# Seven products instead of eight on both column pairs of a split-precision MLP, on one core

## The chip, the cores and the metric

The kernel runs on one core of one Trainium2 chip. The number that counts is the time of one execution in microseconds (us), as the device measures it; the kernel before was run three times, and its median is the reference. A profile of one further execution shows each instruction on each engine: TensorE (PE, with its weight loads PEld), VectorE (DVE), ScalarE (ACT), GpSimd (POOL), and SyncE (SP), which here only issues transfers.

## The reference

A decoder trunk of two layers on 256 tokens of width 2048, all in float32. Layer 0 has recurrent mixers, layer 1 a dilated attention; each is followed by an MLP with 8192 hidden columns. The change lies in the MLP and in how weights are brought to the matmuls:

```python
def squared_relu_mlp(h, w1, w2):
    return jnp.square(jax.nn.relu(h @ w1)) @ w2

for layer in range(DEPTH):
    hn = rms_norm(h, norm_mix[layer])
    ...
    h = h + mix
    h = h + squared_relu_mlp(rms_norm(h, norm_mlp[layer]), mlp_w1[layer], mlp_w2[layer])
return rms_norm(h, final_norm)
```

## The kernel before

**Precision by three matmuls.** Each float32 operand is held as two parts, `hi` (the value rounded to the matmul's input type) and `lo` (the rest), and a product is computed as hi·hi + hi·lo + lo·hi. The parts of the activations live in `bufa` and `bufb` (columns 0 to 255 hi, 256 to 511 lo). The parts of the weights are made on the fly by `Weights.split`: ACT casts a loaded block to `hi` (line 105), DVE subtracts it from the raw block to get `lo` (line 106).

**Units.** All weights are cut into units of 128 partitions x 2048 floats, 1 MB each. The list `units` is the order in which PE needs them. `unit` hands out the next one and calls `fetch` for the one two places ahead, which issues the load on SP's queue (line 123) and the split. The raw blocks have 3 buffers (`wraw`); `hi` and `lo` each have 5 half-unit tiles of 128x1024, thus two and a half units. A scheduler sets the order on each engine; `stream()` and `urgent()` give priorities; the order of the main matmuls among themselves is chained by `mm`.

**The MLP.** The 8192 hidden columns are done in four quarters `q`, in both layers. In a quarter, 16 units of `w1` each give one block of 128 hidden features for all tokens (`project`, `cross`: 16 matmuls of 512 columns and 16 of 256); the result is folded, squared after the relu and split into `bufb` (lines 229 to 242 and 684 to 687). Then 16 units of `w2` take the 16 blocks of the quarter to the output: four column blocks `n` of 512 output columns, two token halves `j`, 16 feature blocks `k`.

**The products.** For the first column pair (n = 0 and 1, as `PAIRS = 1`), the first 8 feature blocks are taken as a two-by-two block product in Strassen's manner: with two token halves, two column blocks and pairs of feature blocks there are seven block products of 12 matmuls each instead of eight. They need sums of activations, which `sums` makes into the tile `forms` during the w1 stage (four sums for each of four pairs of blocks, split into hi and lo), and sums of weights, which `combine` makes on DVE (line 147): `a` becomes a+t1, then a+t1+t2, then that plus d; and `t1` becomes t1+t2 for the product called `t3`. The tiles `a` and `t1` have one buffer each in the pool `pair`. The other 8 feature blocks of the pair are done plainly, in the units called `n`, 24 matmuls each. `PRODUCTS` is the order of the eleven units of a pair; `times` runs the matmuls; `to_x` adds a finished bank to the residual `xres` (the tile `xall`) on DVE (line 657) and, in the last quarter, calls the norm's square on ACT (line 295). The second column pair (n = 2 and 3) is done plainly by `tokens` (192 matmuls for 8 units), and `add_res` adds it (line 592).

**Turning the residual.** At the end of the last quarter of layer 0 each of the four 512-column blocks of the residual is transposed by PE, eight transposes of 128x128 (line 186), scaled and split into `bufa` by ACT and DVE (lines 240 and 241) for the attention's projections. `to_features` puts the work on the list `later`; `flush` runs the list after the next unit of matmuls. As `mlp` calls `products` for two column blocks and only then `to_features`, blocks 0 and 1 come into one flush. The transposes have two banks of PSUM, `pl`.

In the built program `forms` lies at byte 182,048 of its partition in layer 0 and at 186,144 in layer 1; neither is a multiple of 64. `bufa`, `bufb`, `hi` and `lo` lie on multiples of 64.

Of the kernel before, what the change touches and what calls it, by code (L numbers as in the profile page):

```python
# [40 lines left out]
def trunk_kernel(ctx, tc, x, xtok, cols, tab, masks, pos, fin, w_in, w_gate, w_out, w_qkv, w_o, w1, w2, out):  # L41
# [2 lines left out]
    cst = pool("cst")  # L44
    act = pool("act")
    wraw = pool("wraw", 3)
    whi = pool("whi", 5)
    wlo = pool("wlo", 5)
    tmp = pool("tmp", 2)
    mixers = ExitStack()  # L50
    pmm = pool("pmm", 3, space=PSUM)
# [6 lines left out]
    xall = act.tile([P, KB * S], F32, name="xall")  # L58
    xin = xall.rearrange("p (k s) -> p k s", s=S)
    xres = xall.rearrange("p (j d) -> p j d", j=2)  # L60
    bufa = act.tile([P, KB, 2 * S], F32R, name="bufa")
    bufb = act.tile([P, KB, 2 * S], F32R, name="bufb")

    units = []
    made = {}
# [1 line left out]
    def plan(src, n):  # L67
        units.extend((src, i) for i in range(n))
# [13 lines left out]
    units.extend((w_out, 4 * n + g) for n in range(4) for g in (2, 3, 0, 1))  # L82
    for layer in range(2):
        if layer:
            plan(w_qkv, 48)
            plan(w_o, 16)
        for q in range(4):
            units.extend((w1, layer * 64 + q * 16 + i) for i in range(16))
            for n in range(0, 4, 2):
                plan2(layer * 64 + q * 16 + 4 * n, n < 2 * PAIRS)  # L90
    at = [0, 0]

    class Weights:
        def __init__(self, raw, now=True):
            self.raw = raw
            self.hi = [whi.tile([P, 1024], F32R, name="hi") for _ in range(2)]
            self.lo = [wlo.tile([P, 1024], F32R, name="lo") for _ in range(2)]
            if now:
                self.split(0, 1024)
                self.split(1024, 1024)  # L100

        def split(self, at, n):
            h, l = self.part(at, n)
# [2 lines left out]
            V.tensor_tensor(l, w, h.bitcast(F32), OP.subtract)  # L106

        def part(self, at, n):
            i, r = divmod(at, 1024)
            return self.hi[i][:, r:r + n], self.lo[i][:, r:r + n]  # L110

    def fetch():
        u = at[0]
        if u >= len(units):
            return
        at[0] += 1
        src, i = units[u][:2]
        with stream():
            if len(units[u]) > 2:
                combine(u, src, i, units[u][2])  # L120
                return
            r = wraw.tile([P, 2048], F32, name="raw")
            nc.sync.dma_start(r, src[i])
            made[u] = Weights(r)

    held = {}

    def combine(u, src, i, what):
        if what in ("a", "t1"):
            r = held[what] = pair.tile([P, 2048], F32, name=what)  # L130
            nc.sync.dma_start(r, src[i])
        elif i is not None:
            r = wraw.tile([P, 2048], F32, name="raw")
            nc.sync.dma_start(r, src[i])
            held[what] = r
        to, add = {"t1": ("a", "t1"), "t2": ("a", "t2"), "t3": ("t1", "t2"), "t4": ("a", "d"),
                   "a": ("a", None), "c": ("t2", None), "d": ("d", None), "n": ("n", None)}[what]
        r = held[to]
        if what == "t3" and T3_DMA:
            nc.gpsimd.dma_start(r, w2[held["c_at"]], accum_op=OP.add)  # L140
            add = None
        if what == "t2":
            held["c_at"] = i
        for h in range(2):
            at = slice(h * 1024, h * 1024 + 1024)
            if add:
                V.tensor_tensor(r[:, at], r[:, at], held[add][:, at], OP.add)
            if h == 0:
                w = made[u] = Weights(r, False)
            w.split(h * 1024, 1024)  # L150

    def fetch_first():
        for u in range(4):
            at[0] += 1
            r = wraw.tile([P, 2048], F32, name="raw")
            src, i = units[u]
            n = (4, 2, 1, 1)[u]
            for m in range(n):
                ks = slice(4 * u + m * 4 // n, 4 * u + (m + 1) * 4 // n)
                ws = slice(m * 2048 // n, (m + 1) * 2048 // n)  # L160
                nc.sync.dma_start(xin[:, ks], x[:, ks])
                nc.sync.dma_start(r[:, ws], src[i][:, ws])
                if m == 0 and n > 1:
                    made[u] = Weights(r, False)
                for k in range(ks.start, ks.stop):
                    split_to(bufa[:, k], xin[:, k], col("nmix0", k))
                if n > 1:
                    made[u].split(m * 2048 // n, 2048 // n)
                else:
                    made[u] = Weights(r)  # L170

    def unit(src, i):
        u = at[1]
# [90 lines left out]
    class FirstNorm:  # L264
# [2 lines left out]

        def add(self, blk):
            self.n += 1
            q = tmp.tile([P, S], F32, name="n1", bufs=2)  # L270
            A.activation(q, blk, AF.Square)
            if self.n == 1:
                self.ss.append(tmp.tile([P, S], F32, name="ssq", bufs=1))
                V.tensor_copy(self.ss[0], q)
            elif self.n < KB:
                V.tensor_tensor(self.ss[0], self.ss[0], q, OP.add)
            else:
                self.ss.append(q)
# [65 lines left out]
            flush()  # L344
        return ps

    def tokens_group(src, i0, rt=None, by_k=False):
        ps = tokens(src, i0, bufa, by_k=by_k)
        v = vgs.tile([P, 2, 512], F32, name="vg", bufs=2)
        with urgent():  # L350
            for j in range(2):
                A.activation(v[:, j], ps[j], AF.Copy, scale=1.0 if rt is None else rt[:, j:j + 1])
        return v
# [73 lines left out]
        scaled(p, z, acc)  # L427
        return z

    vgs = mixers.enter_context(tc.tile_pool(name="vgs", bufs=2))  # L430
    wk = mixers.enter_context(tc.tile_pool(name="wk", bufs=2))


# [92 lines left out]

    def lru_in(b):
        p = project(w_in, b, bufa, XA)
        xp = wk.tile([P, S + 4], F32, name="xp", bufs=2)
        V.memset(xp[:, :4], 0.0)  # L530
        scaled(p, xp[:, 4:], XA)
        A.activation(xc[:, b], xp[:, 4:], AF.Identity, bias=col("conv_b", b), scale=col("conv_w", 24 + b))
        for i in range(3):
            V.scalar_tensor_tensor(xc[:, b], xp[:, 1 + i:1 + i + S], col("conv_w", 8 * i + b), xc[:, b],
                                   op0=OP.mult, op1=OP.add)
        split_to(bufb[:, b], xc[:, b])
# [93 lines left out]
        A.copy(forms[:, k, 0], t)  # L630
        V.tensor_tensor(forms[:, k, 1], t, forms[:, k, 0].bitcast(F32), OP.subtract)

    def products(i0, n0, nrm, r2, r2n):
        n1 = n0 + 1
        i0 += 4 * n0
        plain = lambda j, k: (bufb[:, k, j * P:j * P + P], bufb[:, k, S + j * P:S + j * P + P])
# [28 lines left out]
        for what, u in PRODUCTS:  # L665
            w = unit(w2, None if u is None else i0 + u)
            if what != "n":
                times(bank[what], w, side[what])
                for job in after_product.get(what, ()):
                    to_x(*job)  # L670
                continue
            n, g = divmod(u, 4)
            for j in (1, 0) if n else (0, 1):
                times({(0, 0): gamma, (0, 1): beta, (1, 0): alpha, (1, 1): delta}[n, j], w,
                      lambda i, j=j, g=g: plain(j, 4 * g + i))
                if g == 3:
                    to_x({(0, 0): gamma, (0, 1): beta, (1, 0): alpha, (1, 1): delta}[n, j], j, n + n0, 1, (n, j) != (1, 1))
            flush()

    def mlp(layer, nrm, nxt, gname):  # L680
        r2 = None
        for q in range(4):
            for m in range(16):
# [7 lines left out]
                if r2 is None:  # L691
# [4 lines left out]
                        lut(spare, epsc, AF.Sqrt)  # L696
                    spot[:] = [after(V.memset(spare, 0.0), [])]
            ends = nxt if q == 3 else None
            for n in range(4):
                if n < 2 * PAIRS:  # L700
                    if n % 2 == 0:
                        products(layer * 64 + q * 16, n, ends, r2, r2n)
                else:
                    ps = tokens(w2, layer * 64 + q * 16 + 4 * n, bufb)
                    add_res(ps, n, ends, r2)
                if q == 3:
                    if gname:
                        to_features(n, gname)
                    else:
                        at = slice(n * 512, n * 512 + 512)  # L710
                        with urgent():
                            for j in range(2):
                                V.tensor_tensor(xres[:, j, at], xres[:, j, at], fing[:, at], OP.mult)

    pairs = ExitStack()
    pair = pairs.enter_context(tc.tile_pool(name="pair0", bufs=1))
    forms = pair.tile([P, 4, 2, 512], F32R, name="forms")
    nx1 = Norm()
    mlp(0, nrm, nx1, "nmix1")
    pairs.close()  # L720
# [78 lines left out]
    pend = []  # L799
    for g in range(4):  # L800
        if g < 3:
            vg = tokens_group(w_qkv, g * 12, rt)
        for hd in range(4 * g, 4 * g + 4):
            u0 = g * 12 + (4 if g < 3 else 0) + (hd % 4) * 2
            st = scores(u0)
# [13 lines left out]
    fing = late.tile([P, D], F32, name="fing")  # L819
    nc.sync.dma_start(fing, bass.AP(tensor=fin.tensor, offset=fin.offset, ap=[[0, P], [1, D]]))  # L820
    pair = pairs.enter_context(tc.tile_pool(name="pair1", bufs=1))
    forms = pair.tile([P, 4, 2, 512], F32R, name="forms")
    fnorm = Norm()
    mlp(1, nrm, fnorm, None)
    pairs.close()
    for j in range(2):
# [3 lines left out]
        with urgent():  # L830
# [18 lines left out]
URGENT = 400  # L849
ORDER = "v0 h0 x0 h1 x1 h2 x2 h3 x3 v1 h4 x4 h5 x5 h6 x6 h7 x7 g0 y0 y1 y2 y3 g1 y4 y5 y6 y7"  # L850
WARM = 12
PAIRS = 1
T3_DMA = False
PRODUCTS = (("a", 0), ("t1", 4), ("n", 6), ("t2", 5), ("c", None), ("n", 7), ("t3", None), ("d", 1), ("n", 2),
            ("t4", None), ("n", 3))
NOSYNC = mybir.DependencyInfo(mybir.DependencyClass.NoSync, mybir.DependencyReason.DATA)


# [101 lines left out]
```

## Time and profile before

| | |
|---|---|
| median of 3 runs | 2222.8 us (2221.32 to 2223.05) |
| profiled execution | 2222.9 us, its span from first to last instruction 2221.1 us |
| PE busy | 2201.0 us, 99% of the span, 12100 matmuls and transposes |
| DVE busy | 1603.2 us, 72% |
| ACT busy | 1142.7 us, 51% |
| POOL busy | 1.9 us |
| TensorE clock granted | 0.998 of full speed |
| DMA | 414.53 MB, 187 GB/s in the mean; SP's queue takes 51.6% of the 16 engines' time |

The page of a profile lists busy times, groups of equal instructions (count, busy time, mean duration of one, and the idle time before them with the instruction that ended it), and the chain of work that ended last. A duration in such a row runs from the start of an instruction to its end; as instructions of one engine overlap at their ends, the distance from start to start can be shorter, and for matmuls is much shorter.

### The profile page before, as it was taken

How to read it: one execution, taken by the hardware profiler on the slowest of the kernel's cores; microseconds unless marked ns; L12 is line 12 of the kernel's file. 1: busy time of each engine (PE TensorE's matmuls, PEld its weight loads, DVE VectorE, ACT ScalarE, POOL GpSimd, SP SyncE). 2: the span in 40 equal slices, each digit the busy share in tenths (PEclk: the TensorE clock that was granted, in tenths of full speed). 3: DMA queues.
4: the chain of work that ended last, by engine and by line, in shares of the span. 5: the costliest groups of instructions: out<-in, count | busy, mean ns of one | idle time of the engine just before them, and what ended most of it. 6: DMA issues, size and time to landing. Idle time of an engine off the chain costs nothing.

```text
span 2221.1 us, 30636 instructions
## 1 busy us (share of the span) xinstructions
PE 2201.0 (99%) x12100; PEld 1917.1 (86%) x12100; DVE 1603.2 (72%) x2526; ACT 1142.7 (51%) x1620; POOL 1.9 (0%) x7
## 2 busy tenths in 40 slices
PE   9999999999999999999999999999999999999998
PEld 8999998888888888888788888888888888888886
DVE  7777886578578578578667778556776776785784
ACT  7444485555455455455555445455544554554553
POOL 0000000000000000000000000000000000000000
PEclk9999999999999999999999999999999999999999
DMA  8444446555555554654454454655465455555543
GB/s 311 152 155 169 153 153 236 181 190 193 202 189 183 200 192 169 226 190 148 181 185 170 176 184 159 232 184 184 152 235 198 174 208 194 189 206 190 189 162 123
DMA packets 58720, 414.53 MB, mean 187 GB/s; under 512 B 6528, under 2 KB 7296, under 8 KB 9168
## 3 DMA queue, kind: packets, MB, share of 16 engines
q1 hardware_dynamic: 58320, 412.20, 51.6%
q8 instruction: 95, 1.56, 0.3%
q0 software_dynamic: 256, 0.38, 0.1%
q14 instruction: 49, 0.40, 0.1%
HBM read 410.70 MB, written 2.10 MB: 186 GB/s over the span
## 4 chain that ended last, share of the span: by engine, by line
PE 97%; ACT 1%; DVE 1%; issue 0%; DMA 0%; SPq 0%; ACTq 0%; DVEq 0%
PE p L183 88%; PE pd L183 6%; PE pl L478 1%; PE pl L186 0%; PE pl L774 0%; ACT hi L105 0%; PE po L795 0%; PE pd L787 0%; DMA xall<-in_x 0%; DVE lo L106 0%; DVE bufa L241 0%; ACT L206 0%; ACT bufa L240 0%; PE pd L462 0%; PE pl L773 0%
## 5 line engine op out<-in xcount | busy, mean ns | idle before, releaser
L106 DVE TENSOR_TENSOR lo<-raw,hi 128x1024 fp32r<-128x1024 f32 (+1 forms) x742 | 895.1, 1219 | 474.2 <-ACT hi L105 325.0
L105 ACT CAST hi<-raw 128x1024 fp32r<-128x1024 f32 (+1 forms) x742 | 777.8, 1049 | 776.3 <-PE p L183 660.0
L183 PE MATMUL p<-bufa,hi 128*128 128x512 f32 (+1 forms) x3840 | 858.1, 357 | 2.4 <-DVE bufa L241 2.4
L183 PEld LDWEIGHTS p<-bufa,hi 128*128 128x128 f32 x3840 | 671.6, 189 | 95.0 <-DVE bufa L241 3.8
L183 PE MATMUL p<-hi,bufb 128*128 128x512 f32 x1984 | 621.3, 390 | 0.0
L183 PE MATMUL p<-bufa,lo 128*128 128x256 f32 x3200 | 519.9, 284 | 0.0
L183 PEld LDWEIGHTS p<-bufa,lo 128*128 128x128 f32 x3200 | 451.7, 191 | 12.3
L183 PEld LDWEIGHTS p<-hi,bufb 128*128 128x128 f32 x1984 | 373.1, 188 | 78.4 <-DVE xall L657 1.2
L183 PE MATMUL p<-lo,bufb 128*128 128x512 f32 x992 | 386.5, 390 | 0.0
L183 PEld LDWEIGHTS p<-lo,bufb 128*128 128x128 f32 x992 | 186.5, 188 | 38.2
L183 PE MATMUL p<-hi,bufa 128*128 128x512 f32 x384 | 122.4, 395 | 0.0
L230 ACT COPY t<-p 128x256 f32<-128x256 f32 x128 | 47.6, 372 | 88.7 <-PE p L183 88.7
L105 ACT CAST hi<-a 128x1024 fp32r<-128x1024 f32 x64 | 67.3, 1051 | 46.2 <-PE p L183 20.6
L238 DVE TENSOR_TENSOR bufb<-zp,bufb 128x256 fp32r<-128x256 f32 x128 | 54.2, 423 | 47.1 <-ACT bufb L237 41.3
L183 PEld LDWEIGHTS p<-hi,bufa 128*128 128x128 f32 x384 | 72.1, 188 | 15.5 <-ACT hi L105 0.9
L183 PE MATMUL pd<-hi,bufb 128*128 128x512 f32 x256 | 82.9, 390 | 0.0
L183 PE MATMUL p<-lo,bufa 128*128 128x512 f32 x192 | 76.3, 398 | 1.8 <-DVE lo L106 1.8
L106 DVE TENSOR_TENSOR lo<-a,hi 128x1024 fp32r<-128x1024 f32 x64 | 76.5, 1216 | 0.0
L686 DVE SCALAR_TENSOR_TENSOR zp<-zp 128x256 f32<-128x256 f32 x128 | 54.2, 423 | 3.5
L183 PEld LDWEIGHTS pd<-hi,bufb 128*128 128x128 f32 x256 | 48.1, 188 | 9.8
L237 ACT CAST bufb<-zp 128x256 fp32r<-128x256 f32 x128 | 51.6, 403 | 7.8 <-DVE zp L686 7.8
L232 DVE TENSOR_TENSOR zp<-p,t 128x256 f32<-128x256 f32 x128 | 53.3, 416 | 0.0
(230 smaller groups left out, 1369.8 us busy)
## 6 DMA issues: line engine op xcount, KB each, us to landing
raw<-in_w SPq DMA_DIRECT2D x240, 1024.0 KB, 4.8
raw<-in_w_qkv SPq DMA_DIRECT2D x48, 1024.0 KB, 4.8
raw<-in_w_in SPq DMA_DIRECT2D x46, 1024.0 KB, 4.8
raw<-in_w_out SPq DMA_DIRECT2D x16, 1024.0 KB, 4.8
raw<-in_w_o SPq DMA_DIRECT2D x16, 1024.0 KB, 4.8
a<-in_w SPq DMA_DIRECT2D x8, 1024.0 KB, 4.8
t<-in_w SPq DMA_DIRECT2D x8, 1024.0 KB, 5.5
xall<-in_xtok SPq DMA_DIRECT2D x1, 2048.0 KB, 9.3
```

Of the source, the lines that this page charges most:

```text
L105: A.copy(h, w)
L106: V.tensor_tensor(l, w, h.bitcast(F32), OP.subtract)
L183: chain[:] = [after(T.matmul(*args, **kw), chain)]
L230: A.copy(t, p[:, S:])
L232: V.tensor_tensor(z, p[:, :S], t, OP.add)
L237: A.copy(dst[:, :S], src)
L238: V.tensor_tensor(dst[:, S:], src, dst[:, :S].bitcast(F32), OP.subtract)
L478: T.matmul(pl[:, j], kq[:, js], halves(qp[:, js], c, True), start=True, stop=True)
L686: V.scalar_tensor_tensor(z, z, 0.0, z, op0=OP.max, op1=OP.mult)
```

## The change

1. `PAIRS` goes from 1 to 2: the second column pair of each quarter is done with products too.
2. The order `PRODUCTS` has t4 ahead of the last two plain units, so that both come last.
3. The sum t1+t2 for `t3` is made by a transfer: a DMA on POOL's queue reads the block t2 from memory once more and adds it into the tile `t1` (`accum_op=OP.add`), issued when t2 is fetched.
4. `hi` and `lo` become whole-unit tiles of 128x2048, three buffers each (five halves before). The units of w1 and w2 are cast and subtracted in one instruction of 2048 columns, and weight sums are added in one; units of other weights still in two of 1024.
5. `products` calls `done` for column block n1 after t3 and flushes after t4, and calls it for n0 at its end; so residual blocks are turned singly. The first group of the attention's projections takes its weights in the order 0, 1, 3, 2, as block 3 is now finished ahead of block 2.
6. `forms`, `bufa`, `bufb`, `hi` and `lo` are aligned to 64 bytes: `forms` now lies at 187,328 and 191,424.
7. To make room, `vg` in layer 0 and `xp` have one buffer each instead of two, and the first norm's temporaries share the buffers of `t1` (the fold's temporary) and `q`.

```diff
-    whi = pool("whi", 5)
-    wlo = pool("wlo", 5)
+    whi = pool("whi", 3)
+    wlo = pool("wlo", 3)
...
-            plan(w_qkv, 48)
+            units.extend((w_qkv, i) for i in (0, 1, 3, 2, *range(4, 48)))
...
-        def __init__(self, raw, now=True):
+        def __init__(self, raw, step=2048):
             self.raw = raw
-            self.hi = [whi.tile([P, 1024], F32R, name="hi") for _ in range(2)]
-            self.lo = [wlo.tile([P, 1024], F32R, name="lo") for _ in range(2)]
-            if now:
-                self.split(0, 1024)
-                self.split(1024, 1024)
+            self.hi = whi.tile([P, 2048], F32R, name="hi", align_bytes=LINE)
+            self.lo = wlo.tile([P, 2048], F32R, name="lo", align_bytes=LINE)
+            for at in range(0, 2048, step) if step else ():
+                self.split(at, step)
...
-            made[u] = Weights(r)
+            made[u] = Weights(r, 2048 if src is w1 or src is w2 else 1024)
...
-        if what == "t3" and T3_DMA:
-            nc.gpsimd.dma_start(r, w2[held["c_at"]], accum_op=OP.add)
+        if T3_DMA and what == "t2":
+            nc.gpsimd.dma_start(held["t1"], src[i], accum_op=OP.add)
+        if T3_DMA and what == "t3":
             add = None
-        if what == "t2":
-            held["c_at"] = i
-        for h in range(2):
-            at = slice(h * 1024, h * 1024 + 1024)
-            if add:
-                V.tensor_tensor(r[:, at], r[:, at], held[add][:, at], OP.add)
-            if h == 0:
-                w = made[u] = Weights(r, False)
-            w.split(h * 1024, 1024)
+        if add:
+            V.tensor_tensor(r, r, held[add], OP.add)
+        made[u] = Weights(r)
...
-        v = vgs.tile([P, 2, 512], F32, name="vg", bufs=2)
+        v = vgs.tile([P, 2, 512], F32, name="vg")
...
-    vgs = mixers.enter_context(tc.tile_pool(name="vgs", bufs=2))
+    vgs = mixers.enter_context(tc.tile_pool(name="vgs", bufs=1))
...
-        xp = wk.tile([P, S + 4], F32, name="xp", bufs=2)
+        xp = wk.tile([P, S + 4], F32, name="xp", bufs=1)
...
                 for job in after_product.get(what, ()):
                     to_x(*job)
+                if what == "t3":
+                    done(n1)
+                if what == "t4":
+                    flush()
                 continue
...
             flush()
+        done(n0)
...
-                if q == 3:
-                    if gname:
-                        to_features(n, gname)
...
+                    done(n)
...
-    forms = pair.tile([P, 4, 2, 512], F32R, name="forms")
+    forms = pair.tile([P, 4, 2, 512], F32R, name="forms", align_bytes=LINE)
...
-            vg = tokens_group(w_qkv, g * 12, rt)
+            vg = tokens_group(w_qkv, g * 12, rt, kgs=(0, 1, 2, 3) if g else (0, 1, 3, 2))
...
-PAIRS = 1
-T3_DMA = False
-PRODUCTS = (("a", 0), ("t1", 4), ("n", 6), ("t2", 5), ("c", None), ("n", 7), ("t3", None), ("d", 1), ("n", 2),
-            ("t4", None), ("n", 3))
+LINE = 64
+PAIRS = 2
+T3_DMA = True
+PRODUCTS = (("a", 0), ("t1", 4), ("n", 6), ("t2", 5), ("c", None), ("n", 7), ("t3", None), ("d", 1),
+            ("t4", None), ("n", 2), ("n", 3))
```

More of the change, by code (lines that the diff above doesn't have):

```diff
@@ L60, in trunk_kernel @@
     xres = xall.rearrange("p (j d) -> p j d", j=2)
-    bufa = act.tile([P, KB, 2 * S], F32R, name="bufa")
-    bufb = act.tile([P, KB, 2 * S], F32R, name="bufb")
+    bufa = act.tile([P, KB, 2 * S], F32R, name="bufa", align_bytes=LINE)
+    bufb = act.tile([P, KB, 2 * S], F32R, name="bufb", align_bytes=LINE)
     units = []
@@ L108, in part @@
         def part(self, at, n):
-            i, r = divmod(at, 1024)
-            return self.hi[i][:, r:r + n], self.lo[i][:, r:r + n]
+            return self.hi[:, at:at + n], self.lo[:, at:at + n]
     def fetch():
@@ L163, in fetch_first @@
                 if m == 0 and n > 1:
-                    made[u] = Weights(r, False)
+                    made[u] = Weights(r, 0)
                 for k in range(ks.start, ks.stop):
@@ L169, in fetch_first @@
                 else:
-                    made[u] = Weights(r)
+                    made[u] = Weights(r, 1024)
     def unit(src, i):
@@ L269, in add @@
             self.n += 1
-            q = tmp.tile([P, S], F32, name="n1", bufs=2)
+            q = tmp.tile([P, S], F32, name="t1", bufs=2)
             A.activation(q, blk, AF.Square)
             if self.n == 1:
-                self.ss.append(tmp.tile([P, S], F32, name="ssq", bufs=1))
+                self.ss.append(tmp.tile([P, S], F32, name="q", bufs=1))
                 V.tensor_copy(self.ss[0], q)
@@ L345, in tokens, with tokens_group @@
         return ps
-    def tokens_group(src, i0, rt=None, by_k=False):
-        ps = tokens(src, i0, bufa, by_k=by_k)
-        v = vgs.tile([P, 2, 512], F32, name="vg", bufs=2)
+    def tokens_group(src, i0, rt=None, by_k=False, kgs=(0, 1, 2, 3)):
+        ps = tokens(src, i0, bufa, kgs, by_k)
+        v = vgs.tile([P, 2, 512], F32, name="vg")
         with urgent():
@@ L631, in sums, with products @@
         V.tensor_tensor(forms[:, k, 1], t, forms[:, k, 0].bitcast(F32), OP.subtract)
-    def products(i0, n0, nrm, r2, r2n):
+    def products(i0, n0, nrm, r2, r2n, done):
         n1 = n0 + 1
@@ L698, in mlp, with done @@
             ends = nxt if q == 3 else None
+            def done(n):
+                if ends is None:
+                    return
+                if gname:
+                    to_features(n, gname)
+                else:
+                    at = slice(n * 512, n * 512 + 512)
+                    with urgent():
+                        for j in range(2):
+                            V.tensor_tensor(xres[:, j, at], xres[:, j, at], fing[:, at], OP.mult)
             for n in range(4):
@@ L701, in mlp @@
                     if n % 2 == 0:
-                        products(layer * 64 + q * 16, n, ends, r2, r2n)
+                        products(layer * 64 + q * 16, n, ends, r2, r2n, done)
                 else:
@@ L705, in mlp @@
                     add_res(ps, n, ends, r2)
-                if q == 3:
-                    if gname:
-                        to_features(n, gname)
[L709 to L713, printed above, removed]
+                    done(n)
     pairs = ExitStack()
     pair = pairs.enter_context(tc.tile_pool(name="pair0", bufs=1))
-    forms = pair.tile([P, 4, 2, 512], F32R, name="forms")
+    forms = pair.tile([P, 4, 2, 512], F32R, name="forms", align_bytes=LINE)
     nx1 = Norm()
@@ L821, in trunk_kernel @@
     pair = pairs.enter_context(tc.tile_pool(name="pair1", bufs=1))
-    forms = pair.tile([P, 4, 2, 512], F32R, name="forms")
+    forms = pair.tile([P, 4, 2, 512], F32R, name="forms", align_bytes=LINE)
     fnorm = Norm()
```

## The prediction

> **What bounds the kernel now.** First the page: busy shares, then the slices and the chain that ended last.
>
> ```profile
> PE 2201.0 (99%) x12100; PEld 1917.1 (86%) x12100; DVE 1603.2 (72%) x2526; ACT 1142.7 (51%) x1620; POOL 1.9 (0%) x7
> ...
> PEclk9999999999999999999999999999999999999999
> ...
> PE 97%; ACT 1%; DVE 1%; issue 0%; DMA 0%; SPq 0%; ACTq 0%; DVEq 0%
> ```
>
> PE is on the chain for 97% of the span at full clock. So a matmul taken away shortens the run, unless something makes PE wait in its place. How long a matmul is must be read from the chain in order of time (start, length, what), as the rows' means overlap. One quarter of layer 0, the end of the last quarter, and the turning of the residual:
>
> ```profile
> 690.12 2.75 PE pd L183 x12
> 692.87 8.28 PE p L183 x36
> 701.15 2.80 PE pd L183 x12
> 703.95 8.24 PE p L183 x36
> 712.19 2.79 PE pd L183 x12
> ...
> 2167.11 43.53 PE p L183 x192
> ```
>
> The last line is a plain column pair: 192 matmuls, 43.53/192 = 0.2267 us each, 2.72 us per 12. The lines above it are a product pair: a; t1 and n6; t2; c and n7; t3. With 24 matmuls at 0.2267 (5.44 us) taken off, t1 takes 2.84 and c 2.80; t2 takes 2.80, t3 2.79: the four that load `forms` are 0.35 us longer together than four times 2.72. The pair runs without a gap to 731.31.
>
> Third, what the other engines do in these two stages (windows: length, busy time of PE, PEld, DVE, ACT, POOL, clock, DMA share, GB/s), and the rows that price their work:
>
> ```profile
> 692.00:731.50 39.50, 39.50 (x174) 32.32 (x173) 33.37 (x36) 22.27 (x23) 0.00 (x0) 1.00 0.66 240
> 731.50:774.50 43.00, 43.00 (x192) 35.59 (x191) 21.80 (x20) 16.66 (x16) 0.00 (x0) 1.00 0.55 195
> ```
> ```profile
> L105 ACT CAST hi<-a 128x1024 fp32r<-128x1024 f32 x64 | 67.3, 1051 | 46.2 <-PE p L183 20.6 <-DVE a L147 20.2 <-PE pd L183 4.9
> L106 DVE TENSOR_TENSOR lo<-a,hi 128x1024 fp32r<-128x1024 f32 x64 | 76.5, 1216 | 0.0
> L147 DVE TENSOR_TENSOR a<-a,raw 128x1024 f32<-128x1024 f32 x32 | 38.3, 1216 | 0.0
> L631 DVE TENSOR_TENSOR forms<-sums,forms 128x512 fp32r<-128x512 f32 x32 | 21.9, 684 | 0.0
> L630 ACT CAST forms<-sums 128x512 fp32r<-128x512 f32 x32 | 19.8, 618 | 0.0
> L657 DVE SCALAR_TENSOR_TENSOR xall<-p,nm,xall 128x512 f32<-128x512 f32 x32 | 23.8, 744 | 3.3 <-PE p L183 3.3
> ```
>
> DVE is nearly full beside a product pair (33.4 of 39.5 us) and half idle beside a plain one (21.8 of 43). The change makes the second stage like the first, so DVE is what to watch.
>
> **The change part by part.**
>
> *Matmuls.* A product pair has 7 x 12 + 4 x 24 = 180 matmuls, a plain one 192. Two layers of four quarters: 8 pairs x 12 x 0.2267 = 21.8 us less on PE.
>
> *Alignment.* The four `forms` products of 8 old pairs lose 8 x 0.35 = 2.8 us if the address is what makes them longer; no other tile changes its alignment, and no operand in the stage but `forms` has the longer interval. The new pairs then pay 2.72 as well. Bounds: 0 and 2.8; I take 2.8, since the same instruction with `bufb` in place of `forms` is the nearest row.
>
> *Turning singly.* In the last quarter of layer 0 blocks 0 and 1 come in one flush, 16 transposes into two banks:
>
> ```profile
> PE pl L186 <- DVE bufa L241: 3.1, 1, 3.1
> ```
>
> PE idles 3.1 us there for DVE to empty the banks, and DVE stands behind subtracts. Blocks turned singly need two banks each, which are free. I take 3.1 us off; bounds 0 and 3.1.
>
> *Splits in one piece.* From 512 to 1024 columns the subtract grows by 1216 - 684 = 532 ns and the cast by 433, so one of 2048 takes 1216 + 1064 = 2280 ns and 1051 + 866 = 1917. DVE work of a new pair: 11 subtracts and 3 sums (t1, t2, t4) of 2.28, and 8 `xall` of 0.744: 37.9 us against 180 x 0.2267 = 40.8 of PE. An old pair had 22 x 1.22 + 8 x 1.22 + 8 x 0.744 = 42.6. So DVE can keep up over a pair, with 2.9 us to spare; the old plain stage no longer has to catch up for it.
>
> *But in order, unit by unit.* With three whole tiles, a unit's buffer is freed when PE ends the unit three before it; then come the cast and the subtract, 4.2 us, and 0.2 for PE's last matmul to drain. PE covers that with the two units between: 8.2 us, or 5.4 where both are short or a and t1 stand between. Tight are n7, t4, n2 and n6. Count from PE's start of a: t1 at 2.7, n6 5.4, t2 10.9, c 13.6, n7 16.3, t3 21.8, d 24.5, t4 27.2, n2 29.9, n3 35.4, then a', t1', n6' of the second pair at 40.8, 43.5, 46.2. With DVE's order in the built program and its instructions behind one another, n7's lo is ready about when PE wants it, t4's at 26.2 and n2's 0.8 us early. One place is late: `a` has a single buffer, so a' is loaded only when t4's subtract has read it, at 26.2; the load takes 4.8 (median of such loads), cast and subtract 4.2, to 35.2; the sum a'+t1' on DVE 2.3, its cast and subtract 4.2, to 41.7; then n3's `xall`, a'+t2' and n6's subtract, 0.7 + 2.2 + 2.2: 46.8, against 46.4 (the lo is wanted by a unit's second matmul). Before, `a` had a whole w1 stage to come. So 0.4 to 0.5 us in each of 8 quarters: 4 us. With a load of 5.5 us, as the row of `t` has, it is 1.2 each. Bounds 0 and 9.6 us; I take 4.
>
> *Last quarters.* There ACT also squares (0.63 us eight times a pair) and, in layer 0, DVE takes four 0.48 us splits per turned block, two blocks now beside products and not beside plain tiles: 3.8 us more than the 2.9 to spare. I take 1.5 us for each layer, 3 in all; bounds 0 and 8.
>
> *The accumulating transfer.* No row shows one. It may start when a+t1 is done (some 4 us before PE's a; for the second pair at 37.4), and the cast of t3 wants it at 13.8 (54.6): 17 us of room, and about 4 more until PE waits, as t3's lo would be ready that much early. Lower bound 4.8 us, the plain 1 MB load. Upper bound from POOL's own queue: 257 KB of `tab` landed in 3.9 us, 15.6 us per MB if all of it scaled, and twice that, 31, if it reads two sources at that rate. Its shape (8 KB per partition) is nearer the plain load; I take about 10 and so no wait. Nothing but these transfers is behind it on POOL. Beside it SP's loads share the 16 engines, 66% busy in this stage.
>
> The Trainium skill, "Collectives: The Full Stack", section "The bandwidth ceiling: the fold count and why AG ≠ RS ≠ AR", says that an adding transfer reads two sources per chunk and so runs at half the rate of a copy. By that rule and the row of 4.8 us it would be about 9.6, inside the room, and the sum stays as it is. No run so far shows it.
>
> *Smaller tiles.* With one `vg`, the second group's evacuation waits for head 3's last use; and in the built order head 4's second projection takes the PSUM bank of its first, so PE waits for DVE's read, 0.42 us behind at most one subtract of 1.22 and the drain: 1 us, once. `xp` is reused a head later, some 17 us: nothing.
>
> *Sum.* 21.8 + 2.8 + 3.1 = 27.7 gained; 4 + 3 + 1 = 8 lost; 19.7 net. The profiled execution took 2222.9 us (span 2221.1 and 1.8 around it), the median 2222.8, so it makes no difference which is used: 2203 us.
>
> **The rivals.**
>
> *No loss at all* (0.12): the thin margins are as wide as the error of the extrapolated 2.28; 2222.8 - 27.7 = 2195.
>
> *The address is not the cause* (0.08): `forms` keeps its interval in 16 pairs, 16 x 0.35 = 5.6 us: 2203 + 5.6 = 2209.
>
> *Splits come late in every pair* (0.14): if the whole-tile chain is 1 us late per pair, at n7 and n6, it costs 16 and not 4: 2215. For it: DVE's share beside products, and that a half tile no longer frees at half a unit. Against it: DVE's total leaves 2.9 us per pair, and PE's wait gives DVE time.
>
> *The accumulating transfer is late* (0.16), the way to slower: from 21 us on PE waits at t3 in all 16 pairs. At 31 us it is 16 x 10 = 160 us: 2363; at 23 us it already eats the gain (16 x 2 = 32 over the 19.7). For it: POOL's queue is slower per byte in every row here. Against it: those rows are short lines and fell into the start of the kernel.
>
> **How the numbers follow.** My forecast has 0.50, from 2197 to 2211. A change under 0.2% (4.4 us) can't be told from none. Faster: 0.50 + 0.12 + 0.08 and half of the late splits, 0.77; the same 0.06 and slower 0.01 of the other half; slower with the late transfer 0.17. The range from 2194 to 2222 holds the forecast, both rivals beside it and most of the late splits; it leaves out the late transfer.
>
> **What would show it.** The chain: a second pair of 40.8 us instead of 43.5, and 2.72 for each `forms` product. PE's wait on L186 of 3.1 us gone. A short wait of PE for `lo` at n6 of the second pair, once per quarter. ACT's cast of t1 not waiting for POOL's DMA. Wrong would be: PE waiting at t3; PE waits at n7 or n2 in each pair of over 0.5 us; a cast or subtract of 2048 columns far from 1.92 and 2.28 us.

## The result: 0.2% slower, and the profile after

| | before | after |
|---|---|---|
| median, us | 2222.19 (10 runs, 2221.19 to 2223.05) | 2227.11 (10 runs, 2226.91 to 2228.44) |
| profiled execution, us | 2222.9 | 2227.3 |
| its span, us | 2221.1 | 2225.5 |

The ratio is 1.0023, with a 95% interval of 1.0014 to 1.0031: slower by 4.9 us, where 2203 was predicted, in a range from 2194 to 2222.

The page of after, busy time and the chain that ended last:

```profile
PE 2207.2 (99%) x12004; PEld 1892.6 (85%) x12004; DVE 1673.0 (75%) x2286; ACT 1110.0 (50%) x1364; POOL 15.8 (1%) x23
...
PE 95%; DVE 3%; ACT 1%; DMA 0%; issue 0%; SPq 0%; ACTq 0%; DVEq 0%
```

PE has 96 matmuls fewer, as meant (12100 before), and is busy 6 us longer (2201.0 before). So the matmuls left have become longer. Waits don't explain it: those of PE that the profile lists add up to 7.2 us, and to 9.7 before. Where they became longer is best seen in a stage that the change doesn't touch, `w_out`. Its column groups have 96 matmuls of 512 columns each. The chain in order of time (start, length, what), first of before, then of after; the last line of each is the first quarter's `w1` stage:

```profile
363.09 21.81 PE p L183 x96
...
385.77 21.78 PE p L183 x96
...
431.46 84.92 PE p L183 x487
```
```profile
362.95 22.28 PE p L176 x96
...
386.10 22.27 PE p L176 x96
...
432.70 85.74 PE p L176 x487
```

21.81/96 is 227 ns a matmul, 22.28/96 is 232. The order, the shapes, the clock (0.998) and the work are the same there. What differs in this stage is that `hi` and `lo` are whole-unit tiles, and where the operands stand in memory. The product pairs, in the chain of after:

```profile
529.79 2.81 PE pd L176 x12
532.60 8.37 PE p L176 x36
540.97 2.81 PE pd L176 x12
543.78 2.78 PE p L176 x12
```

12 matmuls take 2.78 to 2.81 us, not 2.72: the same in products from `bufb` as from `forms`.

The diff asks for multiples of 64 bytes for `bufa`, `bufb`, `hi` and `lo`, which had them already. The request still put 64 unused bytes behind `bufa` and 64 more behind `hi`. Before, the byte addresses of all four had the same remainder on division by 4096. After, the remainders of `bufb` and `hi` are 64 bytes further on than that of `bufa`, and that of `lo` is 128 further on.

The table splits the spans by stage, each from its first matmul to that of the next, in us. a_forms, a_swap and b_addr are kernels of the next section.

| stage | before | after | a_forms | a_swap | b_addr |
|---|---|---|---|---|---|
| first (w_in, w_gate) | 334.8 | 334.1 | 335.8 | 335.8 | 333.2 |
| w_out and w_o | 182.2 | 186.1 | 182.2 | 182.2 | 186.0 |
| w_qkv | 290.8 | 293.6 | 290.7 | 290.7 | 293.7 |
| w1, 8 quarters | 717.5 | 724.6 | 717.5 | 717.5 | 724.6 |
| w2, 8 quarters | 695.8 | 687.2 | 678.0 | 672.4 | 709.2 |
| span | 2221.1 | 2225.5 | 2204.1 | 2198.6 | 2246.6 |

The products do save time, 8.6 us in the w2 stages, and 13.8 are given back in `w_out` and `w_o`, `w_qkv` and `w1`, which have no product.

### The profile page after: what moved, and what is told of

Read it like the earlier page. It is cut to its first block, busy times and chain, and to the rows that moved or that the text cites. A ratio compares the mean times of both kernels' runs of the same rounds, so it can differ in the third digit from the quotient of the medians.

```text
span 2225.5 us, 29702 instructions
## 1 busy us (share of the span) xinstructions
PE 2207.2 (99%) x12004; PEld 1892.6 (85%) x12004; DVE 1673.0 (75%) x2286; ACT 1110.0 (50%) x1364; POOL 15.8 (1%) x23
## 4 chain that ended last, share of the span: by engine, by line
PE 95%; DVE 3%; ACT 1%; DMA 0%; issue 0%; SPq 0%; ACTq 0%; DVEq 0%
PE p L176 81%; PE po L176 6%; PE pd L176 5%; DVE lo L105 1%; PE pl L471 1%; ACT hi L104 1%; PE pl L179 0%; DVE a L142 0%; PE pl L777 0%; PE po L798 0%; DMA xall<-in_x 0%; PE pd L790 0%; DMA a<-in_w 0%; DVE bufa L234 0%; PE pd L455 0%
## 5 line engine op out<-in xcount | busy, mean ns | idle before, releaser
L105 DVE TENSOR_TENSOR lo<-raw,hi 128x1024 fp32r<-128x1024 f32 (+2 forms) x486 | 822.1, 1709 | 359.3 <-ACT hi L104 339.2
L104 ACT CAST hi<-raw 128x1024 fp32r<-128x1024 f32 (+2 forms) x486 | 688.3, 1441 | 685.2 <-PE p L176 524.9
L176 PE MATMUL p<-hi,bufb 128*128 128x512 f32 x1408 | 458.0, 395 | 0.2 <-DVE xall L650 0.2
L176 PEld LDWEIGHTS p<-hi,bufb 128*128 128x128 f32 x1408 | 264.4, 188 | 64.1 <-DVE xall L650 3.1
L176 PE MATMUL p<-lo,bufb 128*128 128x512 f32 x704 | 277.8, 395 | 0.3 <-DVE lo L105 0.2
L104 ACT CAST hi<-a 128x2048 fp32r<-128x2048 f32 x64 | 122.0, 1906 | 160.9 <-PE p L176 83.6
L105 DVE TENSOR_TENSOR lo<-a,hi 128x2048 fp32r<-128x2048 f32 x64 | 146.5, 2289 | 55.5 <-ACT hi L104 55.4
L176 PE MATMUL po<-hi,bufb 128*128 128x512 f32 x256 | 85.4, 394 | 0.1
L176 PE MATMUL p<-hi,forms 128*128 128x512 f32 x256 | 85.4, 394 | 0.0
L142 DVE TENSOR_TENSOR a<-a,raw 128x2048 f32<-128x2048 f32 x32 | 73.0, 2282 | 0.0
```

The lines of the kernel that those rows point to most:

```text
L104: A.copy(h, w)
L142: V.tensor_tensor(r, r, held[add], OP.add)
L176: chain[:] = [after(T.matmul(*args, **kw), chain)]
```

## The experiments

**Are the addresses the cause?** Three kernels take the change and the addresses apart. a_forms is after with the alignment asked for `forms` alone, a_noalign with none at all:

```diff
-            self.hi = whi.tile([P, 2048], F32R, name="hi", align_bytes=LINE)
+            self.hi = whi.tile([P, 2048], F32R, name="hi")
...
     forms = pair.tile([P, 4, 2, 512], F32R, name="forms", align_bytes=LINE)
```

> The changed kernel, with the 64-byte alignment asked for `forms` alone. bufa, bufb, hi and lo then start, as before the change, at the same remainder (320) of 4096 bytes, and forms at 320 of 512. Theory: the changed kernel's 512-column matmuls start every 232 ns instead of 227 because bufb, hi and lo were moved by 64 and 128 bytes; then this runs at 227 in all stages, forms included: 6684 x 4.5 ns = 30 us less than 2227, about 2197. Rival: the whole-unit tiles and instructions of 2048 columns slow PE; then the intervals stay at 232 and the time at 2227.

> As the run before, but forms where it falls, at 288 of 512 bytes, 32 of 64. Theory: 227 ns in all 512-column matmuls but those that load forms, which keep 233: 768 x 6 ns = 4.6 us above the run before, about 2202. Rival: 2227, as nothing but addresses differs from the changed kernel.

a_forms took 2206.09 us (4 runs, 2205.96 to 2206.52), against 2222.99 for runs of before in the same session: ratio 0.9927 (0.9910 to 0.9944). That is 21 us under after, so the whole-unit tiles are not the cause, and 9 us over the 2197 expected. a_noalign took 2209.83 in one run. In the chain of a_forms `w_out` is back, and so are the products:

```profile
364.07 21.81 PE p L176 x96
...
528.75 2.72 PE pd L176 x12
531.47 8.17 PE p L176 x36
```

The mean from the start of a matmul to the start of the next (gaps of 300 ns and more left out) is 232.5 ns over the 6684 matmuls of 512 columns in after, 228.0 over before's 6815 and 227.7 over the 6678 of a_forms. After against a_forms, 6684 x 4.8 ns is 32 us of loss. Two things take some of it back: 4561 matmuls of 256 columns are shorter in after (120.2 ns against 121.3, 4.9 us), and PE's listed waits are 7.2 us and not 12.1. That leaves 22, and the spans differ by 21.4; the expected 2197 counted the loss alone. Between a_noalign and a_forms only the products from `forms` differ: 232.8 ns without alignment, 226.7 with it.

The reverse is b_addr: the old kernel, with after's distances.

```diff
+    act.tile([P, 16], F32, name="pad")
     bufb = act.tile([P, KB, 2 * S], F32R, name="bufb")
...
+    pool("gap").tile([P, 16], F32, name="pad2")
     wlo = pool("wlo", 5)
```

> The kernel before with 64 unused bytes between bufa and bufb and 64 more between hi and lo, so that bufa, bufb, hi and lo stand to one another as they do after the change: nothing else is changed. If the distances alone make the matmuls longer, the intervals become those of after (about 232 ns at 512 columns, 120 at 256): 6815 x 4.5 ns = 30.7 us more, 4479 x 1.4 ns = 6.3 less, and some 3 less for waits that the longer matmuls cover: 2222.8 + 21 = 2244 (2238 to 2248). If the longer interval of after came from something else in it (whole tiles, three buffers, the second products), the time stays within 3 us of 2222.8, or goes down as it did with 64 bytes in one place.

It took 2248.36 us (4 runs): ratio 1.0116 (1.0099 to 1.0133). This is just over what was expected: the waits that longer matmuls were to cover did not shrink (9.8 us listed, and 9.7 before). Its chain at the same places reads as after's:

```profile
362.08 22.27 PE p L185 x96
...
431.82 85.74 PE p L185 x487
```

With 128 unused bytes and no other edit, the old kernel takes on the `w_out`, `w1` and `w_qkv` times of after (the table). So the places of the tiles to one another alone cost it 26.7 us (2248.36 against 2221.7 for before in the same session). That is shown.

**Is it the remainder itself or the distance?** b_all64 puts 64 unused bytes ahead of `bufa`, so that all move together; b_pad64 puts them between `bufa` and `bufb`, so that all but `bufa` move.

```diff
+    act.tile([P, 16], F32, name="pad")
     bufa = act.tile([P, KB, 2 * S], F32R, name="bufa")
```

> The kernel before, with 64 unused bytes ahead of bufa: bufa, bufb, hi and lo all start at 384 of 4096. If equal remainders count, 227 ns everywhere and 2222 us; if the remainder itself counts (64 of 128), 232 and about 2250. Rival (tiles, instructions): 2222.

> The kernel before, with 64 unused bytes per partition between bufa and bufb, so that bufb, hi and lo start at 384 of 4096 and bufa stays at 320. No instruction changes. Theory: slower by up to 30 us, 2240 to 2252. If what counts is that stationary and moving operand have the same remainder, then w1, q and k projections and the first v group (bufa with hi and lo) go to 232 ns and the stages of bufb with hi and lo (w_out, w_o, w2) stay at 227; if it is the remainder itself (64 of 128), all go to 232. Rival (tiles, instructions): 2222, 227 in all.

b_all64 took 2221.57 us, one run: nothing changes when all move together by 64 bytes. b_pad64 took 2212.47, one run too, and that is *faster*, by 10.5, where 2240 to 2252 was expected. In its chain the 28 matmuls of 256 columns after the four on L463 take 3.20 us; in before the like 28 take 3.35. First before, then b_pad64:

```profile
49.56 0.44 PE pd L462 x4
50.01 3.35 PE p L183 x28
```
```profile
48.94 0.44 PE pd L463 x4
49.39 3.20 PE p L184 x28
```

Between `bufa` as moving and `hi` or `lo` as stationary operand, 64 bytes apart, 512 columns take 233.1 ns and not 228.5, but 256 columns take 116.1 and not 121.5. 2541 of the first kind lose 11.7 us, 4479 of the second gain 24.2: 12.5 less, 10.5 measured.

In the same run `hi` and `lo` moved together with `bufb`, and a column group of `w_out`, which has these three as operands, stays at 227 ns a matmul:

```profile
376.97 21.79 PE p L184 x96
```

b_addr has b_pad64's unused bytes and 64 more ahead of `lo`. `hi` and `bufb` stand to one another alike in both, and still the matmuls with these two operands go from 226.9 ns in b_pad64 to 231.9 in b_addr. So the distance between a matmul's own two operands is not all that counts: where `lo`, or a tile behind it, stands matters to matmuls that don't read it.

**At which distances?** a_sweep moves `hi` and `lo` from unit to unit.

```diff
+            off = (made_n[0] // 3 % 4) * 8
+            made_n[0] += 1
-            self.hi = whi.tile([P, 2048], F32R, name="hi")
+            self.hi = whi.tile([P, 2080], F32R, name="hi")[:, off:off + 2048]
```

> The kernel a_forms with 128 unused bytes at the end of each hi and lo tile, so that the three buffers of each stand 128 bytes further on from one another, and with each unit's values starting 0, 32, 64 or 96 bytes into its tile, by turns of three units; one buffer less for two small tiles makes the room. So hi and lo stand 0 to 352 bytes apart from bufa and bufb (modulo 512), in steps of 32. Read from it: the mean interval of matmuls of 512 and of 256 columns by that distance. If the distance counts modulo 128, 0, 128 and 256 give 227 to 228 ns at 512 columns and 121 at 256, and 64, 192 and 320 give 232 to 233 and 116. If only the very same remainder modulo 512 counts, 0 alone gives 227 and 128 and 256 look like 64. The time is then 2206 plus about 4.5 ns for each of some 6700 matmuls of 512 columns at a long distance, less 5 for each of some 4500 of 256 columns: 2206 to 2222.

2221.89 us, one run. Mean intervals in the `w1` and q/k units, in ns, by the distance of `hi` (512 columns) and of `lo` (256 columns) from `bufa` in bytes, modulo 512; 130 to 240 intervals each. `hi` and `lo` move together here, `lo` always 384 bytes further on (modulo 512), so the table doesn't separate what each of them does:

```
distance      0     32     64     96    128    160    192    224    256    288    320    352    384    416    448    480
512 cols  228.7  232.8  233.2  234.4  227.8  233.8  232.9  234.3  232.9  233.3  229.2  233.0
256 cols  121.1  119.8  117.9  117.6  118.9  118.5  114.5  118.6                              120.4  120.4  117.9  117.5
```

Neither expectation holds. At 512 columns 0, 128 and 320 are short and the rest long: 128 isn't like 64, so the very same remainder isn't needed, and 256 and 320 break a period of 128. At 256 columns distance 0, short at 512, is the longest. A rule for the distance stays open.

**The parts of the change, with the addresses held.** b_forms is before with `forms` alone aligned; a_pairs1 is a_forms with `PAIRS = 1`; a_nodma is a_forms with `T3_DMA = False`.

> The kernel before with forms alone on a multiple of 64 bytes. The prediction's term for this is 2.8 us off: 2220. By the intervals measured since (232.8 ns against 226.7 in 384 matmuls) it is 2.3: 2220.5 beside a median of 2222.8. If the shorter interval of forms in a_forms came from something else in that kernel, the time stays.

> The kernel a_forms with products on the first half of the columns only, as before: all else of the change stays. The prediction has 21.8 us for the second pairs, 4 lost in them and part of the 3 of the last quarters: 2206.1 + 21.8 - 4 - 2 = 2222. By the waits seen in the trace of a_forms (0.55 to 0.7 at n6 in most quarters) it is 2206.1 + 21.8 - 5 - 1.5 = 2221. If the second pairs lost nothing it would be 2228; and if it is 2215 or less, the products are worth less than the 12 matmuls that they leave out.

> The kernel a_forms with the third sum on DVE, as before the change, in place of the accumulating DMA; the sum is one instruction of 2048 columns. DVE then has 40.2 us of work in a pair of 40.8 on PE, and each sum stands ahead of the splits of d and t4, of which t4's had 1 us to spare in the prediction's count: 1.3 us late in each of 16 pairs, 2206 + 20 = 2226 (2215 to 2230). If DVE's room is enough all the same, and the transfer saved nothing, 2206 to 2208.

| | us | compared with | difference |
|---|---|---|---|
| b_forms | 2221.06 (10 runs) | before 2222.92 | -1.9 (ratio 0.9992, 0.9982 to 1.0001) |
| a_pairs1 | 2220.55 (1 run) | a_forms 2206.09 | +14.5 |
| a_nodma | 2214.48 (1 run) | a_forms 2206.09 | +8.4 |

The second pairs are worth 14.5 us net, close to the 15 to 16 expected. The interval of b_forms' time just includes no change; its w2 stages are 2.0 us shorter, with 226.7 ns for `forms`. Without the accumulating transfer a pair costs 8.4/16 = 0.5 us more, between the two expectations. PE's waits in a_forms, then in a_nodma (total, times, longest):

```profile
PE p L176 <- DVE lo L105: 5.3, 12, 0.8
...
PE p L176 <- DVE xall L650: 1.6, 8, 0.4
```
```profile
PE p L176 <- DVE lo L105: 8.5, 11, 1.4
PE p L176 <- DVE xall L650: 4.7, 12, 0.7
```

With the third sum on DVE the splits and the reads of the banks both come later.

**The late load of a.** In a_forms the chain at n6 of a second pair reads

```profile
541.62 2.30 DVE lo L105
...
543.94 4.83 DMA a<-in_w
...
548.87 1.92 ACT hi L104
...
550.82 2.30 DVE lo L105
...
553.14 2.30 DVE a L142
...
562.64 2.21 DVE lo L105
...
564.90 5.51 PE p L176 x23
```

t4's subtract, the load of a', its cast and subtract, the sum a'+t1', and at last n6's lo, for which PE waits: the order of the prediction. a_swap exchanges the two buffers in every second pair:

```diff
-            r = held[what] = pair.tile([P, 2048], F32, name=what)
+            pairno[0] += what == "a"
+            r = held[what] = pair.tile([P, 2048], F32, name=("s0", "s1")[(what == "t1") ^ (pairno[0] % 2)])
```

> The kernel a_forms with the two buffers of a and t1 exchanged in every second pair: the second pair's a is loaded into the buffer that t1 had, which is read for the last time by the split of t3, some 10 us before t4's, and t1 waits for t4's in its place. If PE's waits at n6 of the second pair come from the late load of a, as the prediction has it, 7 or 8 waits of 0.55 to 0.7 us go: 2206.1 - 5 = 2201 (2200 to 2203). If they come from the order of work on DVE and ACT, the time stays at 2206 (2205 to 2207).

2200.85 us (4 runs, 2200.71 to 2200.93): ratio 0.9901 (0.9886 to 0.9916), 5.2 under a_forms. In its chain PE goes from the first pair into the second without a wait, and its waits for `lo` fall from 5.3 to 2.1:

```profile
558.70 2.72 PE po L178 x12
561.42 8.18 PE p L178 x36
569.60 2.72 PE po L178 x12
```
```profile
PE p L178 <- DVE lo L105: 2.1, 5, 0.8
```

**A version that beats both kernels.** c_best is a_swap with distances by the width of the matmul: `lo` 64 bytes further on where it is used with 256 columns, and `bufa` 64 bytes lower in the first stage. For room, `hz`, the second layer's `zp` and `fm` have a buffer less.

```diff
+    blocks = lambda at: room[:, at:at + KB * 2 * S].rearrange("p (k c) -> p k c", c=2 * S)
+    bufa = blocks(0)
...
+            shifted = src is w1 or src is w_qkv and (i % 12 >= 4 if i < 36 else i < 44)
...
+    bufa = blocks(16)
     mixers.close()
```

> The kernel a_swap with distances chosen by the width of the matmul: lo stands 64 bytes further on for the units of w1 and of q and k (256 columns), and at the old remainder for all others; bufa stands 64 bytes lower during the first stage, whose projections have 256 columns, and at hi's remainder from then on. To make room, two small tiles have one buffer less. From the intervals by stage: 2500 matmuls of 256 columns with lo from 119.8 to 114.2 ns, 14 us, and 1900 of the first stage from 122.9 to 117.8, 9.7: 2200.9 - 23.5 = 2177 (2174 to 2184). If the first stage and the w1 stages are held by the other engines once PE is faster, half of it or less: 2189 or more.

2190.17 us (4 runs, 2189.89 to 2190.26): ratio 0.9856 (0.9841 to 0.9870), 10.7 under a_swap, half of what was expected. PE's waits are not the reason (10.3 us listed, and 9.1 in a_swap): by stage, 6.0 us came in the first stage, 3.4 in `w1` and 1.3 in `w_qkv`, with the other stages as in a_swap. In the units of `w1` and of q and k the interval of `lo` fell only from 119.8 to 117.9 ns, as at distance 64 in the sweep, and not to b_pad64's 114.4, where `lo` stood 64 from `bufa` too and `hi` did as well; in the first stage it fell from 122.9 to 118.9 and not to 117.8. So here too the distance of one pair of operands doesn't settle its interval. What else does wasn't tried further.

## Why the prediction was wrong, point by point

*The step that failed* is a half sentence of the paragraph on alignment: "no other tile changes its alignment". The four large tiles do stay on multiples of 64, but the prediction took a request for something already so as no edit, and never looked at where the request would put the next tile. So it put the cost of the tiles' places at nothing. They changed relative to one another, and with them nearly every matmul of 512 columns: after is 21.0 us over a_forms, which differs in nothing else. The same paragraph named the address as the likely cause of the longer interval of `forms`, and b_forms bears that out; the rule was held against one tile and not against the others.

*The rest of the sum* gave 19.7 us net; with the addresses undone a_forms is 16.9 under before (2222.99 - 2206.09). That the two are so near is in part luck: layer 0's last quarter gained 2.8 us more than its terms, the six other quarters 4.8 less and layer 1's last 0.8 less. By its terms:

- Matmuls, 21.8: 96 fewer, and 2.72 us for 12 in a_forms. Right.
- `forms`, 2.8: 2.0 in the w2 stages of b_forms. The cause was right, the size somewhat large.
- Turning singly, 3.1: the wait is gone from the list, and layer 0's last quarter is 7.0 us shorter in a_forms (92.3 to 85.3), where the steps give 2.72 + 0.35 + 3.1 - 0.5 - 1.5 = 4.2. The turning itself gave 3.6: from the matmul ahead of the transposes to the one behind them, 16 in one flush took 5.66 us, and 8 take 1.02. The losses of 0.5 and 1.5 hardly came, as PE's listed waits in this quarter of a_forms are 0.4 us in all. Layer 1's is 0.25 shorter (95.3 to 95.1), where they give 1.1.
- The late load of a, 0.5 us a quarter: the place was right, the size too small. The six other quarters fall by 1.8 us (84.7 to 82.9) where 2.72 + 0.35 - 0.5 = 2.6 was expected; a_swap gives back 0.74 a quarter. Of the 0.56 a quarter that is left, the reads of the banks, which the prediction didn't count, hold about 0.2 (`xall`, 1.6 in all); what holds the rest is open.
- Head 4's second projection, 1: 1.0, waiting for `z`, and the first stage is 1.0 longer in a_forms.
- Whole tiles: 2.28 us for a subtract or sum and 1.92 for a cast were extrapolated. The page of after has them:

```profile
L104 ACT CAST hi<-a 128x2048 fp32r<-128x2048 f32 x64 | 122.0, 1906 | 160.9 <-PE p L176 83.6
L105 DVE TENSOR_TENSOR lo<-a,hi 128x2048 fp32r<-128x2048 f32 x64 | 146.5, 2289 | 55.5 <-ACT hi L104 55.4
...
L142 DVE TENSOR_TENSOR a<-a,raw 128x2048 f32<-128x2048 f32 x32 | 73.0, 2282 | 0.0
...
t<-in_w POOLq DMA_DIRECT2D x16, 1024.0 KB, 8.0
```

- The accumulating transfer, estimated at 10 us with 17 of room: it landed in 8.0 (the last line), and PE waits for it nowhere. The rule cited from the Trainium skill, "Collectives: The Full Stack", "The bandwidth ceiling: the fold count and why AG ≠ RS ≠ AR", gives 9.6 from the copy's 4.8. The section states it of collectives, and this is a kernel's own transfer: 8.0 was measured, so the half rate is too low here.

*The rivals.* None was the cause. The transfer wasn't late, the splits weren't late in every pair, and the address was the cause at `forms`. "Slower" was given 0.17, for a mechanism that didn't happen. The waits that were feared are even fewer in after than in a_forms (2.0 us for `lo`, not 5.3), which fits that longer matmuls give DVE more time.

## What to carry to other kernels

Compare the addresses of all tiles in the two builds before costing any edit to a pool, a size or an alignment: a few unused bytes moved this kernel between 2212 and 2248 us. In a kernel that PE bounds, look at a stage that the change doesn't touch, and divide a run of matmuls in the chain by its count; if that differs at the same granted clock, look for something that reaches all stages, as the places of the tiles do. A buffer that is loaded again is freed by its last reader, so where two buffers trade roles, give the next user the one that is free first.

## What the runs showed of the hardware that wasn't expected

The interval of a matmul depends on where the operand tiles stand relative to one another: 226.7 to 228.5 ns against 232 to 234 at 512 columns, and the other way round, 121.5 against 116.1, at 256, at a granted clock of 0.997 to 0.999 in all these runs. Moving all by 64 bytes together changed nothing (b_all64). The distance between a matmul's moving and its stationary operand alone doesn't give the interval: `hi` with `bufb`, at one and the same distance, took 226.9 ns in b_pad64 and 231.9 in b_addr. The Trainium skill, "TensorE: Matmul & The Clock Gate", "Step-by-step: what each phase is for", says that the streaming operand and the weight load have read ports of their own and don't take bandwidth from one another. These runs show some 5 ns per matmul by the places of tiles; whether these two reads meet there, or something else in the memory does it, no run here shows.
